# Inverse roots of the attention's norms: a power on GpSimd in place of a seed and Newton steps on VectorE

## The chip, the core and the metric

The kernel runs on one core of a Trainium2 chip. The metric is the device time of one execution in microseconds (us); the time given for a kernel is the median of its runs. The core has five engines that run their own instruction queues in order: TensorE (PE in the profile; PEld is its weight load), VectorE (DVE), ScalarE (ACT), GpSimd (POOL) and SyncE (SP, which here only issues DMAs). Engines wait for each other through semaphores.

## The reference

One layer of an encoder block on 512 tokens of width 1024. Of its branches the attention matters here: 24 heads of 64 in three groups with dilated windows, whose queries and keys are normalised by their root mean square before the scores.

```python
def rms_norm(x, w):
    xf = x.astype(jnp.float32)
    y = xf * lax.rsqrt(jnp.mean(xf * xf, axis=-1, keepdims=True) + EPS)
    return (y * w.astype(jnp.float32)).astype(x.dtype)
...
    # branch A: bidirectional gated DeltaNet (chunks of 64, a triangular solve per chunk, one scan per direction)
    # branch B:
    q_b = rms_norm(heads(q_b), attn_q_norm_w)
    k_b = rms_norm(heads(k_b), attn_k_norm_w)
    v_b = heads(v_b)
...
    for gi, (window, dil) in enumerate(ATT_GROUPS):
        o_g, l_g = dilated_window_attention(q_b[:, :, gi], k_b[:, :, gi], v_b[:, :, gi],
                                            slopes[gi], dil, window // (2 * dil))
...
    x = x + mixed @ w_o
    # channel mixer: norm, up-projection, centred conv, silu(gate) * up, down-projection
```

So for each token and each head, for the query and for the key, one value `(sum of 64 squares / 64 + EPS) ** -0.5` is needed.

## The kernel before

Each dense product is made of three matmuls (`mm3`, lines 328 to 330): weights and activations are split into a high and a low part, and hi*hi, lo*hi and hi*lo are summed in PSUM. I call such a triple a **block**. The weights arrive by DMA (`wst`), ScalarE writes the high part (`whi`, line 81), and VectorE or, for most weights of the first half, GpSimd subtracts it to get the low part (`wlo`, line 83). From about 660 us to the end only the channel mixer runs, which the change does not touch.

The attention's 24 heads are worked in 12 **units** of two heads (`UNITS`, here numbered 0 to 11). For each unit:
- `att_dense` makes q, k and v of the unit on TensorE, and copies them out of PSUM to `qk` and `v`.
- `att_norms` squares `qk` on ScalarE (line 703), sums each 64 squares on VectorE (line 706, two instructions, to the tile `ass` of 128 partitions by 16), forms the 16 inverse roots per partition (line 710, `newton`: 11 small instructions), multiplies `qk` by them (line 713), and then TensorE transposes q and k (lines 724 and 726) for the scores. I call the first of these transposes **T**.
- `att_softmax` does scores (line 762), exponentials, transposes (799) and values (814).

Besides these run the DeltaNet steps of `chain`: gram matrices (932), decays (523 and 529), an inversion of 32x32 triangles by 31 pairs of VectorE instructions (lines 1011 and 1014, tile `xi`), a round trip through DRAM that spreads the result (a copy at 1020, DMAs at 1022, 1031 and 1035), small matmuls that join the pieces (1049 and 1072), and a scan of eight steps (1099 to 1180).

What sets the order: the kernel is written out in program order by a planner (`Driver`) at build time. Every piece of work books a cost on its engine, `V(n)` for VectorE, `S(n)` for ScalarE, `G(n)` for GpSimd, and `dense` for TensorE. The generators (`att_norms`, `chain` and so on) are stepped when the planner's clock says that what they have issued is done. Instructions of an engine are then run in just this order. The bookings:

```python
    def V(self, n, k=1):
        self.charge("V", k * max(0.28, 0.08 + n * 1.2e-3))
        return self.nc.vector
...
    def G(self, n):
        self.charge("G", 0.15 + n * 2.2e-3)
        return self.nc.gpsimd
```

So a booking changes where everything stands that the planner places later. The functions that the diff touches, and what calls them:

Of the kernel before, what the change touches and what calls it, by code (L numbers as in the profile page):

```python
# [10 lines left out]
F32 = mybir.dt.float32  # L11
# [3 lines left out]
ALU = mybir.AluOpType  # L15
# [7 lines left out]
EPS = 1e-6  # L23
# [97 lines left out]
class Driver:  # L121
# [18 lines left out]
# [4 lines that stand above are left out]
    def S(self, n, k=1):  # L144
        self.charge("S", k * (0.2 + n * 0.83e-3))
        return self.nc.scalar
# [5 lines that stand above are left out]
    def pe(self, us):  # L152

        self.now += us
        self.ready = max(self.ready, self.now) + 0.2
        self.end = max(self.end, self.ready)
# [66 lines left out]
def hybrid(tc, A, out):  # L223
    nc = tc.nc
    ctx = ExitStack()

    def pool(stack, name, side=None, **kw):
        kw.setdefault("reuse_waits", "tile")
        if side:
            kw["side"] = side  # L230
        return stack.enter_context(tc.tile_pool(name=name, bufs=1, **kw))
# [3 lines left out]
    V, S, G, pe = drv.V, drv.S, drv.G, drv.pe  # L235
    cp = pool(ctx, "cp")
# [10 lines left out]
    def small_ps():  # L247
        return pg.tile([128, 512], F32, name="gps", tag="g")
# [4 lines left out]
    def t2(name):  # L253
        return tp.tile([128, T], F32, name=name, tag="t2", bufs=6)
# [5 lines left out]
    def newton(y, x, tmp, scale, bias):  # L260

        n = x.shape[-1]
        V(n).tensor_scalar(x, x, scale, bias, op0=ALU.mult, op1=ALU.add)
        V(n).tensor_scalar(y.bitcast(I32), x.bitcast(I32), -0.5, float(0x5f3759df), op0=ALU.mult, op1=ALU.add)
        for _ in range(3):
            V(n).tensor_mul(tmp, x, y)
            V(n).scalar_tensor_tensor(tmp, tmp, -0.5, y, op0=ALU.mult, op1=ALU.mult)
            V(n).scalar_tensor_tensor(y, tmp, 1.5, y, op0=ALU.add, op1=ALU.mult)

    vec = cp.tile([128, V_END], F32, name="vec")  # L270
    con = cp.tile([128, C_END], F32, name="con")
    ident = con[:, C_ID:C_ID + 128]
    nc.sync.dma_start(vec, A["vec"])
# [96 lines left out]
    def rownorm():  # L370
# [11 lines left out]
        for i in range(4):  # L382
# [9 lines left out]
                                   op0=ALU.mult, op1=ALU.mult)  # L392
# [302 lines left out]
    def att_norms(u, qk):  # L695
        g, p = UNITS[u]
        if g == 0:
            stats[p] = ap_.tile([128, 3, 4, 2, 2], F32, name="stat", tag="stat", bufs=4)
        yield from drv.room(T2, 2)
        ss = ap_.tile([128, 3, 16], F32, name="ass", tag="ass", bufs=2)  # L700
        sqs = [t2("asq").rearrange("p (i c) -> p i c", i=2) for _ in range(2)]
        for i in range(2):
            S(512).activation(sqs[i], qk[:, 2 * i:2 * i + 2], AF.Square)
        yield
        for i in range(2):
            V(512).tensor_reduce(ss[:, 0, i * 8:i * 8 + 8], sqs[i].rearrange("p i (a c) -> p i a c", c=64),
                                 axis=AX.X, op=ALU.add)
        drv.give(T2, 2)
        yield
        newton(ss[:, 1], ss[:, 0], ss[:, 2], 1.0 / 64, EPS)  # L710
        yield
        qk4 = qk.rearrange("p i (a c) -> p i a c", c=64)
        V(1024).tensor_tensor(qk4, qk4, ss[:, 1].rearrange("p (i a) -> p i a", a=4)[:, :, :, None]
                              .to_broadcast([128, 4, 4, 64]), ALU.mult)
        yield "pe"
        while u and not flags.get(("scores", u - 1)):
            yield 0.5
        pad = 64 if g == 0 else 0
        yield from drv.room(PG, 2)
        qT = ap_.tile([128, 2, T], F32R, name="qT", tag="qT", bufs=1)  # L720
        kT = ap_.tile([128, 2, T + 128], F32R, name="kT", tag="kT", bufs=1)
        pq, pk = small_ps(), small_ps()
        for i in range(4):
            nc.tensor.transpose(pq[:, i * 128:(i + 1) * 128], qk[:, i, 0:128], ident)
        for i in range(4):
            nc.tensor.transpose(pk[:, i * 128:(i + 1) * 128], qk[:, i, 128:256], ident)
        pe(1.0)
        kh, kl = kT[:, 0, pad:pad + T], kT[:, 1, pad:pad + T]
        if g == 0:
            G(64).memset(kT[:, :, 0:64].bitcast(F32), 0.0)  # L730
            G(64).memset(kT[:, :, 576:640].bitcast(F32), 0.0)
        S(512).activation(qT[:, 0], pq, AF.Copy)
        S(512).activation(kh, pk, AF.Copy, scale=wqk)
        yield -0.4
        V(512).tensor_tensor(qT[:, 1], pq, qT[:, 0].bitcast(F32), ALU.subtract)
        V(512).scalar_tensor_tensor(kl, pk, wqk, kh.bitcast(F32), op0=ALU.mult, op1=ALU.subtract)
        drv.give(PG, 2)
        flags["qk", u] = qT, kT
        yield
        flags["split", u] = True  # L740
# [456 lines left out]
    def norms():  # L1197
        for u in range(12):
            while u not in soft:
                yield 0.3  # L1200
            yield from att_norms(u, soft[u][0])
# [350 lines left out]
```

## Time and profile before

| | |
|---|---|
| median of 3 runs | 1029.64 us (1028.17 to 1029.99) |
| the profiled execution | 1029.56 us, of which the span of the trace is 1027.8 us |
| TensorE busy | 992.8 us (97% of the span) |
| VectorE busy | 683.7 us (67%) |
| ScalarE busy | 436.1 us (42%) |
| GpSimd busy | 254.1 us (25%), nearly all of it before 560 us |

TensorE's busy time is close to the span, so a change of time shows as waits of TensorE that go or come, or as stretches in which its clock is granted at half speed (1.2 instead of 2.4 GHz). Busy time of the other engines counts only where TensorE waits for them.

### The profile page before, as it was taken

What the parts mean: (1) busy time and instruction counts of PE and PEld (TensorE: products, weight loads), DVE (VectorE), ACT (ScalarE), POOL (GpSimd) and SP (SyncE); (2) the same over time, 40 slices, a digit from 0 to 9 for tenths busy, and PEclk for the clock granted to TensorE, in tenths of its full rate; (3) what the DMA queues carried; (4) which work ended last, traced back from release to release, by engine and by line L of the source; (5) the groups of instructions that cost most, each with busy time, mean ns of one, the idle gap of its engine ahead of it and who ended that gap; (6) DMA issues with size and microseconds to landing.
All of it is one profiled execution on the core that took longest, in us unless ns stands there. A gap on an engine that the chain in (4) does not pass through costs nothing.

```text
span 1027.8 us, 17036 instructions
## 1 busy us (share of the span) xinstructions
PE 992.8 (97%) x6625; PEld 835.3 (81%) x6625; DVE 683.7 (67%) x1134; ACT 436.1 (42%) x864; POOL 254.1 (25%) x229
## 2 busy tenths in 40 slices
PE   8999998989999989999999999999999999999998
PEld 7887888878999878888777877788888888888886
DVE  7569868788988737756857675577776226777621
ACT  6375544584455442433454234244343113344410
POOL 4444376544444433535340001100000000000000
PEclk9999899999999989999999999999999999999999
DMA  6322233373333931312375455222333312323331
GB/s 212 93 87 77 80 123 121 100 187 123 89 94 88 237 82 56 118 49 82 103 256 155 133 166 170 85 82 93 95 101 106 116 66 83 103 82 103 112 113 41
DMA packets 80144, 114.61 MB, mean 112 GB/s; under 512 B 32608, under 2 KB 45120, under 8 KB 79680
## 3 DMA queue, kind: packets, MB, share of 16 engines
q1 hardware_dynamic: 77184, 108.29, 35.2%
q10 hardware_dynamic: 2880, 5.24, 1.3%
q8 instruction: 52, 0.85, 0.3%
q14 instruction: 28, 0.23, 0.1%
HBM read 101.04 MB, written 12.47 MB: 110 GB/s over the span
## 4 chain that ended last, share of the span: by engine, by line
PE 43%; DVE 4%; DMA 2%; ACT 2%; issue 1%; POOL 0%; SPq 0%; POOLq 0%; ACTq 0%; DVEq 0%
PE dps L328 14%; PE dps L330 14%; PE dps L329 14%; DVE wlo L83 1%; DMA wst<-in_wb 1%; DMA xo<-dob 1%; DVE ga L1373 1%; DMA ga<-dgt 1%; DMA wst<-in_wa 1%; ACT mh L1374 0%; DVE gb L1371 0%; PE gps L762 0%; ACT sq L1397 0%; PE gps L1122 0%; ACT whi L81 0%
## 5 line engine op out<-in xcount | busy, mean ns | idle before, releaser
L83 POOL TENSOR_TENSOR wlo<-wst,whi 128x384 fp32r<-128x384 f32 (+2 forms) x152 | 186.4, 1236 | 267.9 <-ACT whi L81 247.2
L81 ACT ACTIVATE whi<-wst 128x384 fp32r<-128x384 f32 (+3 forms) x258 | 175.6, 694 | 174.4 <-PE dps L329 78.7
L328 PE MATMUL dps<-h2h,whi 128*128 128x512 f32 x352 | 139.2, 395 | 0.0
L330 PE MATMUL dps<-h2h,wlo 128*128 128x512 f32 x352 | 139.0, 395 | 0.0
L329 PE MATMUL dps<-h2l,whi 128*128 128x512 f32 x352 | 139.0, 395 | 0.0
L83 DVE TENSOR_TENSOR wlo<-wst,whi 128x1024 fp32r<-128x1024 f32 (+1 forms) x106 | 116.4, 1106 | 21.5 <-ACT whi L81 21.3
L441 ACT ACTIVATE cy<-pre,vec 128x512 f32<-128x512 f32 x56 | 40.3, 724 | 128.9 <-DVE pre L438 128.0
L328 PE MATMUL dps<-whi,hr 128*128 128x384 f32 x256 | 90.9, 355 | 0.0
L329 PE MATMUL dps<-wlo,hr 128*128 128x384 f32 x256 | 86.9, 339 | 0.0
L330 PE MATMUL dps<-whi,lr 128*128 128x384 f32 x256 | 86.9, 339 | 0.0
L330 PEld LDWEIGHTS dps<-h2h,wlo 128*128 128x128 f32 x352 | 66.1, 188 | 16.1
L328 PEld LDWEIGHTS dps<-h2h,whi 128*128 128x128 f32 x352 | 66.1, 188 | 16.0
L329 PEld LDWEIGHTS dps<-h2l,whi 128*128 128x128 f32 x352 | 66.1, 188 | 15.9
L328 PE MATMUL dps<-ah,whi 128*128 128x512 f32 x176 | 69.8, 397 | 0.0
L329 PE MATMUL dps<-al__7562,whi 128*128 128x512 f32 x176 | 69.6, 396 | 0.0
L330 PE MATMUL dps<-ah,wlo 128*128 128x512 f32 x176 | 69.2, 393 | 0.0
L443 DVE SCALAR_TENSOR_TENSOR cy<-pre,vec,cy 128x511 f32<-128x511 f32 x56 | 43.6, 779 | 36.3 <-ACT cy L441 36.3
L1450 DVE TENSOR_TENSOR x<-x,dps 128x512 f32<-128x512 f32 x16 | 11.0, 687 | 78.8 <-PE dps L330 78.8
L785 ACT ACTIVATE sb<-sb,stat 128x128 f32<-128x128 f32 (+1 forms) x96 | 40.7, 426 | 34.3 <-DVE stat L774 34.2
L328 PE MATMUL dps<-hr,whi 128*128 128x512 f32 x120 | 50.7, 422 | 2.8 <-ACT v L684 1.6
L328 PE MATMUL dps<-hh,whi 128*128 128x512 f32 x112 | 46.9, 419 | 4.5 <-ACT hh L292 2.6
L328 PEld LDWEIGHTS dps<-whi,hr 128*128 128x128 f32 x256 | 48.3, 189 | 3.0 <-issue 1.4
(293 smaller groups left out, 2117.9 us busy)
## 6 DMA issues: line engine op xcount, KB each, us to landing
wst<-in_wb SPq DMA_DIRECT2D x66, 512.0 KB, 3.6
wst<-in_wa SPq DMA_DIRECT2D x96, 256.0 KB, 2.7
wst<-in_wa SPq DMA_DIRECT2D x88, 192.0 KB, 2.4
xk<-in_xt SPq DMA_DIRECT2D x24, 256.0 KB, 3.7
dgt<-gt ACTq DMA_DIRECT2D x16, 256.0 KB, 2.0
alb<-daw SPq DMA_DIRECT2D x24, 128.0 KB, 4.1
dg<-dgd SPq DMA_DIRECT2D x16, 128.0 KB, 3.0
ga<-dgt SPq DMA_DIRECT2D x8, 256.0 KB, 5.6
```

The source lines that it names most:

```text
L81: self.drv.S(w).activation(hi[:, :w], st[:, :w], AF.Copy)
L83: eng(w).tensor_tensor(lo[:, :w], st[:, :w], hi[:, :w].bitcast(F32), ALU.subtract)
L328: nc.tensor.matmul(ps, wh, xh, start=first, stop=False)
L329: nc.tensor.matmul(ps, wh, xl, start=False, stop=False)
L330: nc.tensor.matmul(ps, wl, xh, start=False, stop=last)
L441: S(512).activation(y, pre, AF.Copy, scale=w[1])
L443: V(512).scalar_tensor_tensor(y[:, 1:], pre[:, :-1], w[0], y[:, 1:], op0=ALU.mult, op1=ALU.add)
L785: S(w, 1.15).activation(sbs[b, h][:, t], sbs[b, h][:, t], AF.Exp, bias=st[:, 0:1], accum_out=st[:, 1:2])
L1373: nc.vector.tensor_tensor(a, a, b, ALU.add)
L1450: V(512).tensor_tensor(x1[:, d], x1[:, d], ps, ALU.add)
```

## The change

The 16 inverse roots of a unit are no longer formed by `newton` on VectorE. GpSimd scales and adds EPS in one instruction and raises to the power -0.5 in another, whose second operand is a tile of -0.5. `newton` stays in use in three other places.

```diff
     vec = cp.tile([128, V_END], F32, name="vec")
+    mhalf = cp.tile([128, 16], F32, name="mhalf")
+    nc.gpsimd.memset(mhalf, -0.5)
     con = cp.tile([128, C_END], F32, name="con")
...
                                  axis=AX.X, op=ALU.add)
         drv.give(T2, 2)
         yield
-        newton(ss[:, 1], ss[:, 0], ss[:, 2], 1.0 / 64, EPS)
+        G(16).tensor_scalar(ss[:, 0], ss[:, 0], 1.0 / 64, EPS, op0=ALU.mult, op1=ALU.add)
+        G(1250).tensor_tensor(ss[:, 1], ss[:, 0], mhalf, ALU.pow)
         yield
         qk4 = qk.rearrange("p i (a c) -> p i a c", c=64)
```

The planner books 0.19 and 2.90 us on GpSimd for the two, where `newton` booked 11 times 0.28 = 3.08 us on VectorE. Since this frees its VectorE and fills its GpSimd, it places most of what follows differently. Lines of the changed kernel are 2 higher than before from line 270 on, and 3 higher from line 711 on.

GpSimd's queue at unit 2 (`ass` is the tile of sums and roots, `cx` and `qd` are the masks of the gram matrices, `kT` the transposed keys). Before:

```order
L948 TENSOR_TENSOR cx<-cx,sm 128x512
L950 TENSOR_TENSOR qd<-qd,con 128x512
L83 TENSOR_TENSOR wlo<-wst,whi 128x384 x3
L730 MEMSET kT 128x2x64
L731 MEMSET kT 128x2x64
```

And now:

```order
L951 TENSOR_TENSOR cx<-cx,sm 128x512
L953 TENSOR_TENSOR qd<-qd,con 128x512
L712 TENSOR_SCALAR ass<-ass 128x16
L713 TENSOR_TENSOR ass<-ass,mhalf 128x16
L83 TENSOR_TENSOR wlo<-wst,whi 128x384 x3
L733 MEMSET kT 128x2x64
L734 MEMSET kT 128x2x64
```

The two new instructions wait for the sums of line 708 and stand ahead of the next low parts of weights.

VectorE's queue behind the sums of unit 6, near the end of the inversion. Before, from the end of the Newton steps on:

```order
L1011 TENSOR_TENSOR tmp<-lt,xi 128x270
L1014 TENSOR_TENSOR xi<-xi,tmp 128x2x5x27
L713 TENSOR_TENSOR qk<-qk,ass 128x1024
L854 COPY nstat<-stat 128x16
L1011 TENSOR_TENSOR tmp<-lt,xi 128x224
L1014 TENSOR_TENSOR xi<-xi,tmp 128x2x4x28
L1011 TENSOR_TENSOR tmp<-lt,xi 128x174
L1014 TENSOR_TENSOR xi<-xi,tmp 128x2x3x29
```

And now, from the sums on:

```order
L708 TENSOR_REDUCE ass<-asq 128x8 x2
L1014 TENSOR_TENSOR tmp<-lt,xi 128x174
L1017 TENSOR_TENSOR xi<-xi,tmp 128x2x3x29
L1014 TENSOR_TENSOR tmp<-lt,xi 128x120
L1017 TENSOR_TENSOR xi<-xi,tmp 128x2x2x30
L857 COPY nstat<-stat 128x16
L716 TENSOR_TENSOR qk<-qk,ass 128x1024
L1014 TENSOR_TENSOR tmp<-lt,xi 128x62
L1017 TENSOR_TENSOR xi<-xi,tmp 128x2x31
```

The inversion's steps stand some four steps further ahead in relation to the unit. When the unit's `qk` is multiplied, one step is left, where five were left before; the steps with 270 and 224 elements now stand ahead of the sums.

TensorE's queue where the joining matmuls begin (`dps` with `whi`, `wlo`, `hr`, `lr` is the dense work of a later unit, `qT` and `kT` are those of unit 7). Before, 21 blocks behind T of unit 7:

```order
L328 MATMUL dps<-whi,hr 128x384
L329 MATMUL dps<-wlo,hr 128x384
L330 MATMUL dps<-whi,lr 128x384
L762 MATMUL gps<-kT,qT 128x128 x24
L1049 MATMUL gps<-cx 32x32
L1049 MATMUL gps<-aux,cx 32x32
```

And now, right at T of unit 7:

```order
L727 MATMUL gps<-con,qk 128x128 x4
L729 MATMUL gps<-con,qk 128x128 x4
L330 MATMUL dps<-whi,hr 128x384
L331 MATMUL dps<-wlo,hr 128x384
L332 MATMUL dps<-whi,lr 128x384
L1052 MATMUL gps<-cx 32x32
L1052 MATMUL gps<-aux,cx 32x32
```

The joining moved up by 20 blocks and the scores of a unit against T, and is in front of the exponentials and scores of units 6 and 7 that preceded it.

## Rows read from the trace of the kernel before

**Rows 1.** The page's busy times, and the granted clock in 40 slices.

```profile
PE 992.8 (97%) x6625; PEld 835.3 (81%) x6625; DVE 683.7 (67%) x1134; ACT 436.1 (42%) x864; POOL 254.1 (25%) x229
PEclk9999899999999989999999999999999999999999
```

**Rows 2.** Who TensorE waited for: total us, times, longest.

```profile
PE gps L724 <- DVE qk L713: 5.1, 4, 2.9
PE gps L529 <- DVE pre L523: 2.0, 1, 2.0
PE dps L330 <- DVE wlo L83: 1.2, 1, 1.2
```

**Rows 3.** Newton instructions on VectorE, grouped: busy us, mean ns | idle before.

```profile
L266 DVE TENSOR_TENSOR ass<-ass 128x16 f32<-128x16 f32 x36 | 13.2, 365 | 1.2
L268 DVE SCALAR_TENSOR_TENSOR ass<-ass 128x16 f32<-128x16 f32 x36 | 12.6, 349 | 1.2
L267 DVE SCALAR_TENSOR_TENSOR ass<-ass 128x16 f32<-128x16 f32 x36 | 11.8, 327 | 1.2
L264 DVE TENSOR_SCALAR ass<-ass 128x16 int32<-128x16 int32 x12 | 7.0, 587 | 0.4
L263 DVE TENSOR_SCALAR ass<-ass 128x16 f32<-128x16 f32 x12 | 5.1, 428 | 0.0
```

**Rows 4.** Groups of GpSimd, same columns.

```profile
L83 POOL TENSOR_TENSOR wlo<-wst,whi 128x384 fp32r<-128x384 f32 x88 | 98.5, 1127 | 143.8 <-ACT whi L81 140.5 <-PE gps L799 2.3 <-PE dps L329 0.8
L83 POOL TENSOR_TENSOR wlo<-wst,whi 128x512 fp32r<-128x512 f32 x56 | 77.7, 1396 | 107.0 <-ACT whi L81 92.1 <-issue 8.4 <-PE dps L330 5.6
L619 POOL MEMSET sm<- 128x64 f32 x2 | 0.2, 163 | 0.0
```

**Rows 5.** VectorE in order of time in unit 0's Newton steps: start, us.

```profile
80.78 1.18 DVE L266 TENSOR_TENSOR ass<-ass 128x16 f32<-128x16 f32 x1
81.99 1.22 DVE L267 SCALAR_TENSOR_TENSOR ass<-ass 128x16 f32<-128x16 f32 x1
83.25 1.22 DVE L268 SCALAR_TENSOR_TENSOR ass<-ass 128x16 f32<-128x16 f32 x1
84.50 0.17 DVE L266 TENSOR_TENSOR ass<-ass 128x16 f32<-128x16 f32 x1
```

**Rows 6.** GpSimd in order of time, same stretch.

```profile
80.63 3.80 POOL L83 TENSOR_TENSOR wlo<-wst,whi 128x512 fp32r<-128x512 f32 x3 [1.18 <-ACT whi L81]
85.43 2.70 POOL L83 TENSOR_TENSOR wlo<-wst,whi 128x512 fp32r<-128x512 f32 x2 [1.00 <-ACT whi L81]
```

**Rows 7.** VectorE at unit 1: the sums, first Newton instruction, the multiplication.

```profile
147.12 1.28 DVE L706 TENSOR_REDUCE ass<-asq 128x8 f32<-128x512 f32 x2 [1.92 <-ACT asq L703]
...
149.64 0.65 DVE L263 TENSOR_SCALAR ass<-ass 128x16 f32<-128x16 f32 x1
...
157.03 1.22 DVE L713 TENSOR_TENSOR qk<-qk,ass 128x1024 f32<-128x1024 f32 x1
```

**Rows 8.** TensorE in order of time: T of unit 1.

```profile
158.30 1.06 PE L724 MATMUL gps<-con,qk 128*128 128x128 f32 x4 [2.92 <-DVE qk L713]
```

**Rows 9.** Busy times in stretches: PE, PEld, DVE, ACT, POOL, granted clock, DMA, GB/s.

```profile
103.80:110.60 6.80, 6.80 (x23) 5.83 (x23) 5.81 (x18) 3.15 (x10) 1.16 (x3) 0.50 0.26 74
158.40:161.80 3.40, 3.40 (x14) 3.40 (x15) 3.37 (x5) 2.42 (x6) 1.70 (x3) 0.50 0.09 25
190.00:340.00 150.00, 144.65 (x939) 131.14 (x936) 134.09 (x237) 84.45 (x208) 67.97 (x62) 1.00 0.43 123
```

**Rows 10.** VectorE in order of time: unit 6 and the inversion's end.

```profile
315.80 1.28 DVE L706 TENSOR_REDUCE ass<-asq 128x8 f32<-128x512 f32 x2
...
320.91 1.22 DVE L713 TENSOR_TENSOR qk<-qk,ass 128x1024 f32<-128x1024 f32 x1
...
332.34 0.22 DVE L1014 TENSOR_TENSOR xi<-xi,tmp 128x62 f32<-128x62 f32 x1
...
336.00 2.28 DVE L1020 COPY xt__3724<-xi 128x2048 f32<-128x2048 f32 x1
```

**Rows 11.** SyncE's queue: the DMA out and the last DMA back.

```profile
338.31 0.32 SPq L1022 DMA_DIRECT2D dx<-xt__3724  x1
...
360.74 0.46 SPq L1035 DMA_DIRECT2D aux<-dx  x1
```

**Rows 12.** TensorE in order of time: T of unit 7 and the joining matmuls.

```profile
349.35 0.65 PE L724 MATMUL gps<-con,qk 128*128 128x128 f32 x4 [0.22 <-DVE qk L713]
...
365.04 0.21 PE L1049 MATMUL gps<-cx 32*32 32x32 f32 x1
...
368.05 0.21 PE L1049 MATMUL gps<-cx 32*32 32x32 f32 x1 [1.81 <-ACT og L820]
```

## The prediction

> **What bounds the kernel now.** I read the page first. TensorE is busy for 992.8 of 1027.8 us [rows 1], so some 35 us at most are waits; a further loss hides in the slices in which the granted clock falls. VectorE is the next, and in the stretch from 190 to 340 us it is busy for 134.1 of 150 us (89%) [rows 9]: there it is nearly full, though TensorE is fuller. Then I asked whom TensorE waited for. The list is short: 5.1 us in four waits of a T (the first transposes of a unit) for the multiplication by the inverse roots, 2.0 us at the decays' matmuls (line 529), and no row at all for a low weight part made by GpSimd; the one late `wlo` (1.2 us) came from VectorE [rows 2]. So what the change can take away directly is small: those 5.1 and 2.0 us, and whatever half-clock stretches hang on them.
>
> **What is removed.** Twelve times 11 VectorE instructions. Their groups sum to 13.2 + 12.6 + 11.8 + 7.0 + 5.1 = 49.7 us [rows 3], 4.1 us a unit. They do not cost that by themselves: one alone takes 0.17 us, and beside a running GpSimd subtraction 1.18 to 1.22 us [rows 5]. Three such long ones in a row stand exactly beside three subtractions that take 3.80 us together [rows 6]: the small instruction ends when the GpSimd instruction ends. Undisturbed, a unit would take 11 x 0.17 = 1.9 us.
>
> **What is added.** On GpSimd a scaling of 16 elements and a power of 16 elements, 12 times, and a memset of 0.16 us at the start [rows 4], where all wait for DMA anyway. The trace has no power. From below its bound is the cheapest instruction of GpSimd near that size, 0.16 us; from above I set, as an estimate, twice what the planner books for it, 5.8 us. I take the booking, 2.9 us: where the planner's GpSimd rule can be held against rows it is near (384 elements book 0.99 and take 1.13, 512 book 1.28 and take 1.40) [rows 4], and 16 elements of a plain operation would never have been booked as 1250. With 0.2 us for the scaling and on average half a subtraction (0.6 us) until GpSimd is free, the roots are there 3.7 us behind the sums. Before, from the sums to the multiplication, unit 1 took 157.03 - 148.40 = 8.6 us [rows 7], unit 6 320.91 - 317.08 = 3.8 us [rows 10]; both include other VectorE work of 2 to 3 us that stood between.
>
> GpSimd's 12 x 3.1 = 37 us lie in its idle time: it waits 250.8 us in front of the two large groups of subtractions alone [rows 4]. The two new instructions wait for the sums, and the next low weight parts queue behind them. No wait of TensorE for such a part exists now, so I charge nothing; without that cover each unit could cost up to 3 us.
>
> **What VectorE really gains.** During a power, a VectorE instruction with two operands in SBUF should be held as the small ones are held now [rows 5, 6], and the inversion (lines 1011 and 1014), which fills VectorE between units 3 and 6, consists of just those. Where other work is next, the queue soon reaches the multiplication and waits there for the power. Either way VectorE loses about 2.8 us per unit, so of 49.7 us only 49.7 - 12 x 2.8 = 16 us are gained, and if the power blocked nothing, all of it. The rule for this is in the Trainium skill, "SBUF — State Buffer", section "Who interferes with whom": VectorE and GpSimd share a port pair by an exclusive lock that is held for a whole instruction, and a VectorE instruction with two SBUF inputs contends with a GpSimd one that reads SBUF. The trace agrees (1.2 against 0.17 us); by that rule the gain is the 16 us, without it 49.7.
>
> **Where the gain meets TensorE.**
> - T of unit 1. TensorE waits 2.92 us [rows 8], and right behind it the clock is at 0.50 (1.2 GHz) for 3.4 us, TensorE busy all through [rows 9], a loss of 1.7 us. With the roots 3.7 us behind the sums this T is ready some 2.5 to 5 us earlier, and the order now puts 16 gram matmuls ahead of it. I take both away: -4.6 us (bounds 0 and -4.6).
> - The decays' matmuls (529). Their vector work stood behind unit 0's Newton steps and now does not, but is held by unit 0's power, and the planner moved the matmuls up by 3 blocks: -1.0 us (bounds 0 and -2.0).
> - The other T: the planner moved them up by 1 to 8 blocks of 0.5 to 0.7 us, about what the path gains. 0 (from -2.2, what is left of 5.1, to +4).
> - The joining of the inverses. This is what speaks against the change. Before, the copy at line 1020 ended at 338.28, the DMA behind it was issued at 338.31, the last DMA back at 360.74 [rows 10, 11], and the second half of the joining began at 368.05 after a wait of 1.81 us [rows 12]: the data was just in time. Now the joining stands right at T of unit 7, which was at 349.35 and will be some 5 us earlier: it is wanted about 365.04 - 349.35 + 5 - 1 = 20 us earlier. The copy cannot come that much earlier. In the order it stands just behind the multiplication of unit 6, which needs that unit's dense work on TensorE and cannot run ahead of it: 3 us earlier at most than 322.1, then one step and three small operations (1.5 us), the copy's 2.3 us: about 323, 15 us earlier than 338.28. So TensorE waits 20 - 15 = 5 us, less what slack there was in SyncE's queue (22 us from issue to last issue, in which only its own weight loads stand between). I take +3.0 us (bounds 0 and +8).
>
> Sum: -4.6 - 1.0 + 0 + 3.0 = -2.6 us. Against the profiled execution's 1029.56 us, which is 0.08 us from the median, that gives 1027.0 us. Its own range, from the bounds that go together, is 1022 to 1031.
>
> **The rivals.**
> 1. The gain is all taken back (no change). For it: the planner spends the freed VectorE on an earlier place for everything, and T and the joining stand as close to their data as before. Each new wait of 2 to 5 us at a T or at line 1049 cancels one that went. -2.6 plus some 2.6 of such waits: 1029.6 us.
> 2. Slower by the joining. Only the joining's wait decides, at its full 8 us; a TensorE that stands still there has small matmuls around it, and clock stretches at 0.50 of 6.8 us behind such places, like the one at 103.8 us [rows 9], cost 3.4 us more. -5.6 + 8 + 3.4 = +5.8: 1035.4 us. It decides from a wait of about 7.5 us on. Against it: VectorE is nearly full in that stretch, so what is freed there does move the inversion up.
> 3. Slower by the power's length. If it takes 5.8 us, GpSimd's queue stands still for 6 us and more per unit; the low weight parts behind it are late, and the multiplications too. 12 units, of which some half would show 1.5 us at TensorE: -2.6 + 9 = +6.4: 1036.0 us. Against it: GpSimd waits for ScalarE most of the time, so it is ahead.
> 4. More than forecast. The joining is in time, and the scan, which now ends 34 blocks earlier in TensorE's order (behind block 560 instead of 594), no longer shares its end with unit 11. -5.6 with some 3 us of the later waits gone: 1021 us.
>
> **How the numbers follow.** 0.2% of this time is 2.06 us, about what a measurement can tell. Chances: the forecast 0.46, within which 0.36 lie beyond 2.06 us and 0.10 within; rival 1 0.17; rival 2 0.16; rival 3 0.11; rival 4 0.10. Faster: 0.36 + 0.10 = 0.46. Same: 0.10 + 0.17 = 0.27. Slower: 0.27. The range goes from 1020 us, a little under rival 4, to 1036 us, where the rivals on the slow side lie; it leaves out some 0.1 on each side.
>
> **What would show it.** In the changed profile: a power of 2.5 to 3.5 us, 12 times; VectorE's two-operand instructions up to 3 us long beside it, its busy time lower by 15 to 25 us only; T of unit 1 without a wait, and no clock of 0.50 right behind it; a wait of 2 to 6 us at the first or the second half of the joining (now line 1052), where there was 1.81; no row of TensorE waiting for GpSimd's `wlo`. I am wrong if the power is far from 3 us, if the inversion ends later than about 325 us (then rival 2), or if waits for low weight parts appear (rival 3).

## The result and the profile after

The changed kernel takes 1038.76 us (median of 4 runs, 1037.65 to 1041.21), the kernel before 1029.27 us beside it: a ratio of 1.0086 with an interval of 1.0061 to 1.011. It is slower by about 9 us, 0.9%. In the changed kernel `mm3` is at lines 330 to 332, the sums are at 708, the scaling at 712, the power at 713, the multiplication at 716, T at 727 and the joining at 1052 and 1075. In the kernels of the experiments the lines from the power on stand up to 5 further down again.

The page's span, busy times and granted clock in 40 slices, which answer to [rows 1]:

```profile
span 1035.8 us, 16927 instructions
...
PE 993.2 (96%) x6625; PEld 837.6 (81%) x6625; DVE 653.2 (63%) x1002; ACT 437.1 (42%) x864; POOL 294.7 (28%) x254
...
PEclk9999998989999969999999999999999999999999
```

The span grew by 8.0 us, and TensorE's busy time by 0.4: span less busy time, which I call TensorE's idle time below, went from 1027.8 - 992.8 = 35.0 to 1035.8 - 993.2 = 42.6 us. So the loss is waiting. It is not more work, and on balance not work at a lower clock either, since the busy time would hold both. VectorE is busy 30.5 us less, GpSimd 40.6 us more. What was to be freed was freed; TensorE waits more all the same. For whom it waits, to be held against [rows 2]:

```profile
PE gps L727 <- DVE qk L716: 11.2, 5, 5.1
PE dps L330 <- ACT v L686: 5.9, 1, 5.9
PE gps L1052 <- DVE qt L1058: 5.1, 1, 5.1
...
PE gps L1077 <- DVE cx L1085: 1.4, 1, 1.4
```

Of the kernel before, these rows belong beside them, with the 1.81 us of [rows 12]:

```profile
PE dps L328 <- ACT v L684: 2.0, 2, 1.6
PE gps L1072 <- issue: 1.8, 1, 1.8
```

The waits of a T went from 5.1 to 11.2 us. The waits for the joining are 5.1 + 1.4, where there were 1.8 + 1.8. And one wait is of a kind that the prediction does not speak of: 5.9 us in front of a block of the dense work (the one behind 264 blocks in TensorE's order, below "block 264"), which waits until ScalarE has copied `v` out of PSUM; the same place waited 1.6 us before. The 2.0 us at the decays' matmuls (529) are gone. Together +6.1 + 4.3 + 2.9 - 2.0 = +11.3 us; the idle time grew by 7.6, so smaller waits, those of the scan among them, fell by the rest.

The tile of the sums and roots, `ass`: duration in ns (least, median, most), then who sat idle for it and who waited.

```profile
L712 POOL TENSOR_SCALAR ass<-ass x12: 204/205/526, 83.6 to 515.1; 128x16 f32<-128x16 f32 x12
L713 POOL TENSOR_TENSOR ass<-ass,mhalf x12: 2901/2910/3339, 83.9 to 515.3; 128x16 f32<-128x16 f32 x12
L716 DVE TENSOR_TENSOR qk<-qk,ass x12: 1216/2016/2307, 88.9 to 518.3; 128x1024 f32<-128x1024 f32 x12
its engine sat idle before it (us, times) until:
  POOL ass L713: 14.0, 7
```

The power takes 2.91 us. VectorE stood still for it 14.0 us in 7 units, and the multiplication behind it now mostly takes 2.0 us instead of 1.2 [rows 7]: it starts when the power ends, and so does the low weight part that was queued behind the power on GpSimd.

**T of unit 1.** GpSimd in order of time (start, us, engine, line):

```profile
150.22 1.50 POOL L951 TENSOR_TENSOR cx<-cx,sm 128x512 f32<-128x512 f32 x1
151.67 1.75 POOL L953 TENSOR_TENSOR qd<-qd,con 128x512 f32<-128x512 f32 x1
153.50 0.53 POOL L712 TENSOR_SCALAR ass<-ass 128x16 f32<-128x16 f32 x1
154.11 3.23 POOL L713 TENSOR_TENSOR ass<-ass,mhalf 128x16 f32<-128x16 f32 x1
```

and VectorE and TensorE beside it:

```profile
146.74 0.68 DVE L708 TENSOR_REDUCE ass<-asq 128x8 f32<-128x512 f32 x1
...
157.38 2.00 DVE L716 TENSOR_TENSOR qk<-qk,ass 128x1024 f32<-128x1024 f32 x1 [2.08 <-POOL ass L713]
```
```profile
159.53 1.09 PE L727 MATMUL gps<-con,qk 128*128 128x128 f32 x4 [5.10 <-DVE qk L716]
```

The sums end at 147.42. GpSimd is not free then: it runs the masks of the gram matrices (951, 953) and low weight parts, in the order in which they are written, and comes to the scaling at 153.50. The roots are there at 157.34, 9.9 us behind the sums, and T waits 5.10 us where it waited 2.92 [rows 8].

**The wait at block 264.** ScalarE, then VectorE, in order of time. `xk`, `hr` and `lr` are a rewriting of the activations by classes (lines 312, 317, 319); `sb` and `stat` are the scores of unit 2.

```profile
224.31 1.12 ACT L317 ACTIVATE hr<-xk 128x512 fp32r<-128x512 f32 x1 [0.75 <-DVE xk L312]
...
226.18 0.36 ACT L686 ACTIVATE v<-dps,rtok 64x128 f32<-64x128 f32 x1
```
```profile
216.96 0.68 DVE L775 SCALAR_TENSOR_TENSOR sb<-acon,gps 128x512 f32<-128x512 f32 x1
...
219.59 0.74 DVE L312 SCALAR_TENSOR_TENSOR xk<-xk,vec,rstd 128x512 f32<-128x512 f32 x1
```

ScalarE's copies out of PSUM (684 to 686) stand behind the rewriting (317), which waits for VectorE's line 312, which stands behind the scores that the planner now places ahead of it. Before, six of the eight steps of the rewriting (line 310 there) ran ahead of these scores; now four do, and the copies stand behind the sixth:

```profile
217.02 2.44 DVE L310 SCALAR_TENSOR_TENSOR xk<-xk,vec,rstd 128x512 f32<-128x512 f32 x2
...
221.99 0.67 DVE L772 SCALAR_TENSOR_TENSOR sb<-acon,gps 128x512 f32<-128x512 f32 x1
```

TensorE, whose next block waits for a PSUM buffer that these copies free, starts again at 226.59. No power or root is in this chain.

**The joining.** VectorE's copy (now line 1023) runs at 328.66 for 2.32 us, 7.3 us earlier than at 336.00 [rows 10]. ScalarE, VectorE and TensorE in order of time:

```profile
358.83 0.52 ACT L81 ACTIVATE whi<-wst 128x384 fp32r<-128x384 f32 x1 [4.13 <-DMA wst<-in_wa]
...
362.29 1.05 ACT L1060 ACTIVATE qt<-gps 32x512 f32<-32x512 f32 x2
```
```profile
359.84 1.13 DVE L902 TENSOR_TENSOR og<-og,alb 128x512 f32<-128x512 f32 x1 [5.13 <-DMA alb<-daw]
...
362.89 1.29 DVE L1058 COPY qt<-gps 32x512 f32<-32x512 f32 x2 [1.20 <-ACT qt L1060]
```
```profile
356.31 0.21 PE L1052 MATMUL gps<-cx 32*32 32x32 f32 x1
...
363.63 0.26 PE L1052 MATMUL gps<-aux,cx 32*32 32x32 f32 x1 [5.11 <-DVE qt L1058]
```

TensorE begins the joining at 356.31 without a wait: the inverses are there. It stands still in the middle, until the first results are copied out of PSUM. Both copying engines are late through another DMA: ScalarE's queue stands still for 4.13 us until a weight tile is there, VectorE's for 5.13 us until `alb` is there. SyncE issues these DMAs right behind the last of the round trip:

```profile
353.98 0.84 SPq L1038 DMA_DIRECT2D aux<-dx  x1
354.92 1.01 SPq L67 DMA_DIRECT2D wst<-in_wa  x1
355.97 1.09 SPq L899 DMA_DIRECT2D alb<-daw  x2
```

**The clock** behind two of these waits, one row for each stretch (columns as in [rows 9]):

```profile
361.20:371.40 10.20, 7.77 (x144) 7.61 (x145) 5.21 (x8) 2.83 (x6) 2.88 (x3) 0.50 0.24 74
156.40:163.20 6.80, 3.67 (x15) 3.70 (x16) 5.70 (x11) 2.83 (x5) 6.80 (x8) 0.50 0.25 63
```

TensorE is at 0.50 (1.2 GHz) there. The clock fell while TensorE stood still, so a part of each stretch is the wait itself: at T of unit 1 TensorE is busy for only 3.67 of the 6.8 us.

### The profile page after: what moved, and what is told of

The parts are those of the page before. It is cut to its first block, busy times and chain, and to the rows that moved or that the text cites. A ratio compares the mean times of both kernels' runs of the same rounds, so it can differ in the third digit from the quotient of the medians.

```text
span 1035.8 us, 16927 instructions
## 1 busy us (share of the span) xinstructions
PE 993.2 (96%) x6625; PEld 837.6 (81%) x6625; DVE 653.2 (63%) x1002; ACT 437.1 (42%) x864; POOL 294.7 (28%) x254
## 3 DMA queue, kind: packets, MB, share of 16 engines
q1 hardware_dynamic: 77184, 108.29, 34.1%
## 4 chain that ended last, share of the span: by engine, by line
PE 72%; DVE 7%; issue 7%; POOL 4%; DMA 4%; ACT 4%; SPq 1%; POOLq 0%; ACTq 0%; DVEq 0%
PE dps L330 21%; PE dps L331 21%; PE dps L332 20%; DMA wst<-in_wa 2%; POOL wlo L83 2%; PE gps L765 1%; POOL ass L713 1%; DVE wlo L83 1%; PE gps L817 1%; PE gps L802 1%; DVE qk L716 1%; PE gps L1125 1%; PE gps L1165 1%; DVE xk L312 1%; DMA wst<-in_wb 1%
```

## The experiments

Two things changed at once: the work (a power on GpSimd instead of Newton steps on VectorE) and the order, because the planner now books 0.185 + 2.9 us of GpSimd for the roots instead of 11 x 0.28 = 3.1 us of VectorE. **Theory A**: the order is what costs. With VectorE booked as free, the planner places scores, T and the joining earlier than their data comes. **Theory B**, the rival: the power is what costs, by its length and the queue in which it stands, on the way from the sums to the multiplication. All times below are medians, and each ratio is to the kernel before, measured on the same chip (there 1028.7 to 1029.9 us). The fastest and the slowest run of one kernel lie 0.2 to 1.0% apart, and the medians are of 4 to 12 runs, so what can be told is what the intervals say: some 2 us either way for a ratio, and some 3 us for the difference of two such kernels. A ratio is taken over all runs and can be 0.001 off the quotient of the medians. An idle time is that of one profiled run, which can lie 3 to 4 us off the median. The idle times in the expectations leave out some 3.6 us behind the last matmul, those in my tables don't.

### Work and order apart

The power with the old order: VectorE is booked, nothing runs there.

```diff
-        G(16).tensor_scalar(ss[:, 0], ...)
-        G(1250).tensor_tensor(ss[:, 1], ss[:, 0], mhalf, ALU.pow)
+        V(16, 11)
+        nc.gpsimd.tensor_scalar(ss[:, 0], ...)
+        nc.gpsimd.tensor_tensor(ss[:, 1], ss[:, 0], mhalf, ALU.pow)
```

> The power on GpSimd as in the change, but the planner books what it booked for the Newton steps (11 x 0.28 us on VectorE, nothing on GpSimd), so that every other instruction stands where it stood before. Theory A, the new order is what costs: the 8 to 9 us of the change are gone, 1027 to 1031 us; T of unit 1 may still wait some 3 us. Theory B, the power itself costs, by the hold on VectorE and by GpSimd's queue that stands still: 1035 to 1040 us, as the change.

The Newton steps with the new order:

```diff
-        G(16).tensor_scalar(ss[:, 0], ...)
-        G(1250).tensor_tensor(ss[:, 1], ss[:, 0], mhalf, ALU.pow)
+        keep, drv.charge = drv.charge, lambda e, us: None
+        newton(ss[:, 1], ss[:, 0], ss[:, 2], 1.0 / 64, EPS)
+        drv.charge = keep
+        G(16)
+        G(1250)
```

> The Newton steps on VectorE as before, but the planner books the change's 0.19 and 2.90 us on GpSimd and nothing on VectorE, so that every other instruction stands where the change has it. Theory A (order): as slow as the change or slower, 1037 to 1045 us, since VectorE now also has the Newton steps' 50 us to do in an order that leaves no place for them. Theory B (work): back at 1028 to 1031 us.

A short GpSimd instruction in the power's place, in the new order (`ALU.mult` for `ALU.pow` in the changed kernel; the inverse root is left out):

> The change with a multiplication by the same tile instead of the power; it leaves the inverse root out. About 0.2 us instead of 2.91 us, same queues, same waits, same order. Theory A (the order wants everything earlier than it can be): most of the loss stays, 1034 to 1038 us. Theory B (length of the power): the loss is gone, 1027 to 1031 us. Between, the two share it: T of unit 1 gets its roots 2.7 us earlier and the wait of 5.1 us there falls to 2.4.

The same in the old order, so the first of these edits with `ALU.mult`; the inverse root is left out here too:

> The kernel before's order with the scaling and a multiplication on GpSimd instead of the Newton steps; it leaves the inverse root out. It is the bound for roots that cost nearly nothing in the old order. Both theories: 1023 to 1028 us, the 5.1 us of waits at T and a half-clock stretch less; if it is not under 1028, the Newton steps were hidden anyway, and no faster root could have gained in this order.

In the traces the orders are held exactly: but for the roots' own instructions, TensorE, VectorE and ScalarE run the same instructions in the same order within each of the two columns. Measured, in us; idle is TensorE's, from the page of the profiled run:

| for the roots | old order | idle | new order | idle | new less old |
|---|---|---|---|---|---|
| Newton steps, VectorE | 1029.36 (before) | 35.0 | 1047.74, ratio 1.0189 [1.0166, 1.0212] | 48.7 | +18.4 |
| power, GpSimd | 1024.67, ratio 0.9955 [0.9934, 0.9976] | 29.6 | 1038.76 (the change) | 42.6 | +14.1 |
| 0.2 us on GpSimd | 1017.09, ratio 0.9886 [0.9863, 0.9908] | 23.5 | 1033.38, ratio 1.0046 [1.0029, 1.0063] | 37.1 | +16.3 |

The table is read along both sides. Along a row, the new order costs 14 to 18 us, whatever makes the roots. Down a column, the power gains against the Newton steps, 4.7 us in the old order and 9.0 in the new, and its 2.9 us cost 7.6 or 5.4 us against an instruction of 0.2 us. So both theories name a real cost, but B alone can't make the change slower: the power is dear and still cheaper than what it replaces. The order turns the sign. My ranges were missed all the same: the old order came out faster than I had for A (1024.67 against 1027 to 1031) and for both theories (1017.09 against 1023 to 1028), the Newton steps in the new order slower (1047.74 against 1037 to 1045), and the short instruction there just under A's range (1033.38 against 1034 to 1038). Where A and B differ, each time is nearer to A's range than to B's. And the waits show that the loss needs no slow root. In the new order with Newton steps TensorE waits:

```profile
PE gps L730 <- DVE qk L719: 12.9, 5, 7.5
PE dps L330 <- ACT v L686: 6.0, 1, 6.0
```

with the short instruction:

```profile
PE dps L330 <- ACT v L686: 5.9, 1, 5.9
PE gps L1052 <- DVE qt L1058: 5.0, 1, 5.0
PE gps L727 <- DVE qk L716: 4.7, 2, 2.9
```

and with the power in the old order:

```profile
PE gps L728 <- DVE qk L717: 3.5, 2, 2.2
...
PE dps L330 <- ACT v L686: 1.7, 2, 1.4
```

The 6 us at block 264 stand in the new order whatever makes the roots, and in the old order it is 1.4 us there with the power. The 5 us in the middle of the joining stand there with the power and with the short instruction (2.6 us with Newton steps), and in the old order no wait there is over 1.8 us. At T of unit 1 work and order meet: with the short instruction it still waits 2.9 us, not the 2.4 that I expected, and with the power in the old order 1.3 us, where the scaling has one pair of masks less in front of it and the roots are there 6.1 us behind the sums instead of 9.9:

```profile
145.11 1.28 DVE L708 TENSOR_REDUCE ass<-asq 128x8 f32<-128x512 f32 x2 [1.91 <-ACT asq L705]
```
```profile
149.59 2.92 POOL L714 TENSOR_TENSOR ass<-ass,mhalf 128x16 f32<-128x16 f32 x1
```

### Is it the amount booked, or any other order?

An order made by a planner may be a matter of luck. **Theory C**: every order but the tuned one costs several us. Against it, A says that the amount booked counts. Five bookings were tried; in each, only the lines that book differ.

Power, with both engines booked (`G(16)`, `G(1250)` and `V(16, 11)`):

> The change, but the planner books for the roots both GpSimd's 3 us and the 3.1 us of VectorE that it booked before. Theory A (the loss comes from a booking that leaves VectorE free, so that the first transposes of a unit and the joining are placed before their data): T and the joining are placed as late as before or later, TensorE's idle time is 25 to 29 us, the time 1022 to 1028 us. Theory C (any order other than that of the kernel before costs, whichever way the booking is off): 1031 us or more, TensorE idle 32 us or more, with waits at other places than in the changed kernel.

Newton steps on VectorE as before, booked as 10 or as 12 instructions (`V(16, 10)`, `V(16, 12)`) instead of 11:

> The work of the kernel before, Newton steps on VectorE, with one instruction of the eleven left out of the planner's booking. Theory A: 0.28 us less booked per unit moves little, and a little in the bad direction: 1029 to 1033 us. Theory C (orders are a lottery of several us): 1035 us or more, or 1025 or less.

> The work of the kernel before, with one instruction more in the planner's booking than is done. Theory A: a little later for every T and the joining: 1025 to 1030 us. Theory C: off by 5 us or more in either direction, so about as likely 1035 as 1023.

Power, with 6 or with 16 instructions of VectorE booked (`V(16, 6)`, `V(16, 16)`):

> The power on GpSimd, six instructions of VectorE booked for the roots (1.7 us a unit) instead of eleven (3.1 us). In this order the second pair of score instructions of unit 2 stands ahead of the first rewriting by classes again, as in the changed kernel. If that swap makes the wait at block 264, it is 5 to 6 us here too; T of unit 1 stands between the two orders and waits 2 to 4 us; the time lies between the two, 1029 to 1035 us. If the loss follows the amount booked alone: the same time, but with a wait at block 264 of 2 to 4 us. If all of the booking is needed: 1036 us or more.

> The power on GpSimd, sixteen instructions of VectorE booked (4.5 us a unit), more than the sums need to become roots in most units. If a late place only gives slack back: T and the joining wait nowhere over 1 us and the time is 1021 to 1026 us. If a late place costs as an early one does (work behind T is late for its readers): 1027 us or more, with waits of TensorE for the scores' softmax or the scan.

| work | booked for the roots, per unit | us | ratio | idle |
|---|---|---|---|---|
| power | GpSimd 3.1 us (the change) | 1038.76 | 1.0086 [1.0061, 1.011] | 42.6 |
| power | VectorE 1.7 us | 1032.0 | 1.0025 [1.0011, 1.0038] | 39.0 |
| power | VectorE 3.1 us | 1024.67 | 0.9955 [0.9934, 0.9976] | 29.6 |
| power | VectorE 3.1 us and GpSimd 3.1 us | 1023.75 | 0.9954 [0.9934, 0.9973] | 30.3 |
| power | VectorE 4.5 us | 1031.76 | 1.0025 [1.0011, 1.0038] | 37.1 |
| Newton | VectorE 2.8 us | 1030.25 | 1.0016 [0.9998, 1.0035] | 34.1 |
| Newton | VectorE 3.1 us (before) | 1029.3 | | 35.0 |
| Newton | VectorE 3.4 us | 1030.6 | 1.0019 [1.0, 1.0038] | 33.9 |

C falls: three other orders near the old amount lie within 1.3 us of their kin, the one with both engines booked among them. They are no mere copies of the old order: in their traces 675, 798 and 1342 of TensorE's 6625 matmuls are out of its sequence, where it is 1460 in the changed kernel. With 3.4 us booked I had expected 1025 to 1030 us, a little less than before, and 1030.6 is no gain. Since booking GpSimd beside VectorE changes nothing that can be told (1023.75 against 1024.67), what costs is VectorE's missing booking. A holds on the early side, 1038.8 to 1032.0 to 1024.7 us as the booking grows. It misses on the late side, where I had 1021 to 1026 us as the case that speaks for it: with 4.5 us booked the time is back at 1031.8, and the T's wait nowhere over 1 us, but what comes behind them does:

```profile
PE gps L818 <- DVE pt L808: 4.3, 1, 4.3
PE gps L1126 <- DVE r L1118: 3.7, 1, 3.7
```

These are the values of the softmax and the scan. So a late place costs as an early one does, and of the three amounts tried the best is the one near what the step takes: the power's 2.9 us, for which VectorE's queue can stand still. With 1.7 us booked, VectorE's scores stand ahead of the rewriting again, and the wait at block 264 is there:

```profile
PE gps L728 <- DVE qk L717: 10.1, 4, 6.1
PE dps L330 <- ACT v L686: 5.4, 2, 4.7
```

The 4.7 us lie between the 2 to 4 that the amount alone would give and the 5 to 6 that I had for the swap, and with both engines booked, or Newton steps booked as 12, the wait at this place is 3.4 us although the pair is not swapped. So the swap goes with a long wait each time, and is not all that makes one. T of unit 1 waits 2.9 us here, as expected; the 6.1 us are T of unit 7, which I had not expected.

### Where in the program

The booking of the change from unit 4 on, with the old one before (the two instructions follow without a booking of their own):

```diff
+        if u < 4:
+            V(16, 11)
+        else:
+            G(16)
+            G(1250)
```

> The power on GpSimd; the planner books the old VectorE time for units 0 to 3 and GpSimd's time from unit 4 on. If each misplaced group costs for itself: up to block 290 as in the kernel with the old order (wait at T of unit 1 1.3 us, at block 264 1.4 us), behind it a wait of 4 to 6 us at the joining, 1 to 3 us at T of units 7 and 11 and the half clock behind them: 1030 to 1034 us. If the loss comes from the first units alone: 1024 to 1027 us.

The other way round, with `u > 3` in place of `u < 4`:

> The power on GpSimd; the planner books GpSimd's time for units 0 to 3 and the old VectorE time from unit 4 on. If each misplaced group costs for itself: T of unit 1 waits 5 us, block 264 some 6 us, the joining 2 us or less: 1030 to 1034 us, and its loss and that of the kernel with the two bookings the other way round add up to the 14 us between the changed kernel and the one with the power in the old order. If the loss comes from the joining and the later units alone: 1024 to 1027 us. If a late start makes all later places late too: 1036 us or more.

Measured: 1034.53 us (1.0035 [1.0017, 1.0052]) with the new booking from unit 4 on, 1029.76 us (0.9996 [0.9979, 1.0013]) with it up to unit 3. Above the power in the old order that is +9.9 and +5.1 us, together 15.0 where the whole change has 14.1. By the ratios it is +8.2 and +4.2, together 12.4 where the whole change has 13.5. Within the noise the losses add up, so no first mistake drags the rest along. Their shares are a little off what I expected: by the medians the later half is 0.5 us above its range of 1030 to 1034 (by its ratio inside it), with a wait of only 1.5 us at the joining instead of 4 to 6, and the earlier half is 0.2 us below the same range, although its waits are there in full:

```profile
PE gps L732 <- DVE qk L721: 7.2, 3, 5.2
PE dps L330 <- ACT v L686: 5.9, 1, 5.9
```

By the spans of the two profiled runs the early half costs 8.1 us (1027.8 against 1019.7), by the medians 5.1. The medians are the better measure: the profiled run of the power in the old order, 1021.52 us, lies 3.1 us under the median of its 11 runs. The exact split between the halves stays open by some 3 us.

### What a power costs

The old order, the power as two instructions of 8 elements (against the first of the edits above):

```diff
-        nc.gpsimd.tensor_tensor(ss[:, 1], ss[:, 0], mhalf, ALU.pow)
+        for c in (slice(0, 8), slice(8, 16)):
+            nc.gpsimd.tensor_tensor(ss[:, 1, c], ss[:, 0, c], mhalf[:, c], ALU.pow)
```

> The order of the kernel before, and the power on GpSimd as two instructions of 8 elements each instead of one of 16. If a power costs by its elements: 1.45 us each, VectorE's holds halved, the time as with one instruction, 1023 to 1026 us, or a little less. If it has a fixed price of nearly 3 us: 5.8 us per unit, and the time rises by about the 7.6 us that the short operation gained in this order, to 1030 to 1033 us.

```profile
L715 POOL TENSOR_TENSOR ass<-ass,mhalf x24: 1633/1642/2056, 83.4 to 496.7; 128x8 f32<-128x8 f32 x24
```

1.64 us for 8 elements and 2.91 for 16: (2.91 - 1.64) / 8 = 0.16 us for each element of a partition and 0.37 us besides, if the two sizes lie on a straight line. The time is 1027.73 us (0.999 [0.9974, 1.0006]), 3.1 us above the single power, for 2 x 1.64 - 2.91 = 0.37 us more per unit. The price goes by the elements, but splitting it gains nothing and costs a little: my range for that case, 1023 to 1026, was too low, and halved holds can't help, since there are none (next part).

## Why the prediction was wrong

The forecast was -2.6 us; it came to about +9, beyond rival 3, the slowest of them. What decided is that the sum priced the waits for the roots and for the inverses and left out what else the new order moves: the work alone is -4.7 us, on the side that I forecast, and the order +14.1. By its steps:

- **"I take the booking, 2.9 us"** for the power: right, 2.91 us. So rival 3, which wants 5.8 us, has its condition not met; the 2.9 us alone cost 5.4 to 7.6 us against a short instruction, and still left a gain.
- **"T of unit 1 ... I take both away: -4.6"**: wrong, and the first step that failed. The roots were to be "3.7 us behind the sums", of which 0.6 us was for GpSimd's queue, an average over its idle time. They came 9.9 us behind. GpSimd works through its list in the order written, and at this place the list has masks and weight parts in front; rows of this unit's own place, not an average, were needed. They were at hand: the GpSimd queue shown ahead of the prediction as that of "unit 2" is that of unit 1 in the numbering from 0 (its masks, new instructions, three low parts and memsets run from 150.22 to 161.5 us here), and it has the masks in front of the scaling. T waits 5.10 us, so the term was +2.2 for the wait, not -2.9, and the clock is still at 0.50 there.
- **"The other T ... 0"**: wrong. Their waits went from 5.1 - 2.9 = 2.2 to 11.2 - 5.1 = 6.1 us, just under its upper bound of +4. The planner moved these T up by 1 to 8 blocks, as I had read, but only three of the twelve units had their roots within 3.7 us of the sums; the others had them 4.5 to 9.9 us behind.
- **The decays' matmuls (529) "-1.0"**: the whole 2.0 us went, in the power's old order too, so its lower bound was the value.
- **"The joining ... +3.0"**: the place and the size were right (+2.9 in its waits), the cause was not, so the number is luck. I read the 1.81 us before as data just in time, but the row in [rows 12] names ScalarE's copy of `og` (line 820), so it was not the inverses that TensorE waited for. Two errors then cancelled: the copy began at 328.66, not about 321, and the sign "later than about 325 us" came true; but T of unit 7 was 5.4 us later than before (354.77 against 349.35), not 5 earlier, so the joining was wanted 8.7 us earlier (356.31 against 365.04) instead of 20, and the copy came 7.3 us earlier. The inverses were in time. What was late was the copying of the first results, held up by two other DMAs that stand behind the round trip's in SyncE's queue. With the new booking from unit 4 on, TensorE waits only 1.5 us at the joining and the kernel is still 9.9 us above the power in the old order, so this wait is one of several; rival 2 had it as the only one.
- **What the sum did not have**: the 4.3 us more at block 264, for dense work that has nothing to do with the roots. I listed what waits for the roots, and the change moved everything that is planned behind VectorE's booking. The gain to be had was set too low as well, at "5.1 and 2.0 us" and some half clock: roots of 0.2 us in the old order gain 12.3 us. And the range was cut short: the upper bounds of the four terms add up to +12 us, 1041.6 us, which holds the result, but "the bounds that go together" end at 1031 without a reason.
- **"VectorE loses about 2.8 us per unit ... 16 us are gained"**, "lower by 15 to 25": it was 30.5 us lower, because a power does not hold VectorE. With the short instruction in the same order VectorE is busy 651.8 us, with the power 653.2, though the twelve powers are 32 us longer. VectorE beside GpSimd in unit 4:

```profile
271.24 1.24 DVE L1014 TENSOR_TENSOR tmp<-lt,xi 128x504 f32<-128x504 f32 x1
...
273.23 0.69 DVE L1014 TENSOR_TENSOR tmp<-lt,xi 128x510 f32<-128x510 f32 x1
```
```profile
270.91 1.02 POOL L83 TENSOR_TENSOR wlo<-wst,whi 128x384 fp32r<-128x384 f32 x1 [1.32 <-ACT whi L81]
272.02 0.52 POOL L712 TENSOR_SCALAR ass<-ass 128x16 f32<-128x16 f32 x1
272.62 3.34 POOL L713 TENSOR_TENSOR ass<-ass,mhalf 128x16 f32<-128x16 f32 x1
```

The step beside the subtraction takes 1.24 us; the next one, of the same kind and nearly the same size, runs beside the power in 0.69 us. The 16 us came from carrying the hold of a subtraction over to a power. The Trainium skill, "SBUF — State Buffer", section "Who interferes with whom", says that VectorE's two-input instructions contend with a GpSimd instruction that reads SBUF, and that the port pair is locked for a whole instruction. The subtraction beside line 1014 agrees; the power, which reads SBUF too, does not, and the measurement decides. What VectorE loses to the power is the wait in its own queue, 14.0 us, and the longer multiplications (22.1 us in all against 15.4). That is 6.7 of the 19.2 us between the 49.7 and the 30.5; where the rest lies, no run here separates.
- **No wait for a GpSimd `wlo`**: right within 0.2 us of TensorE's time.

## What to carry to other kernels

In a kernel whose order comes from bookings, an edit changes two things, the work and the order. Price them apart: run the new work under the old booking first, and the old work under the new. An operation moved to a slower, in-order engine keeps its consumer's queue waiting, so book that wait where it is felt as well, at about what the step takes; here that turns 1038.8 us into 1024.7 or 1023.8, and both beat the kernel before. And an idle share of an engine says nothing of whether its queue is free at the moment that counts: read what stands in front at that place.

## What the runs showed of the hardware

- A power on GpSimd takes 2.91 us for 16 elements of a partition and 1.64 us for 8, so 0.16 us for each element and 0.37 us besides if these two sizes lie on a line. A multiplication of 16 elements takes 0.22 us:

```profile
L713 POOL TENSOR_TENSOR ass<-ass,mhalf x12: 220/222/653, 84.8 to 511.1; 128x16 f32<-128x16 f32 x12
```

- The power leaves VectorE's two-input instructions of 128x510 at the 0.69 us that they take undisturbed, while it is itself lengthened a little when it starts while one of that size runs (3.34 and 3.23 us against 2.91). Why, no run here shows.
